# Three weight buffers, a lower part cast one piece later, and chains spread by one tile in a fused decoder layer

## The chip, the cores and the metric

The kernel runs on one core of a Trainium2 chip. The core has a matrix engine (PE, with its weight loads PEld), a vector engine (DVE), a scalar engine (ACT), a general engine (POOL), and a sync engine (SP) that here issues nearly all DMAs. Each engine runs its own instructions in the order in which the program was written, and waits where an operand is not ready. The metric is the device time of the core in microseconds (us); lower is better.

## The reference

One decoder layer on 256 tokens of width 2048, all in float32. A norm of x feeds one wide projection; three branches read it (gated linear attention, attention with a forget gate, attention into 256 memory tokens), each is gated, projected, gated again and summed, and an output projection is added to x.

```python
h = rmsnorm(x, norm_gain[l])
z = h @ w_in[l]
(gq, gk_, gv, ggate, gdown, fq, fk, fv, flogit, fgate,
 mq, mgate, merge) = jnp.split(z, IN_OFFSETS, axis=-1)
gk_log = log_sigmoid(gdown @ w_gk_up[l] + b_gk[l]) / GK_NORMALIZER
o_a = rmsnorm(gla_chunked(gq, gk_, gv, gk_log), gla_norm_gain[l]) * silu(ggate)
log_f = log_sigmoid(flogit + b_f[l])
o_b = forgetting_attention(fq, fk, fv, log_f) * silu(fgate)
mk, mv = jnp.split(rmsnorm(mem, mem_norm_gain[l]) @ w_mem_kv[l], 2, axis=-1)
o_c = memory_attention(mq, mk, mv) * silu(mgate)
y = (gates[:, :, 0] * (o_a @ wb[BRANCH_ROWS[0]:BRANCH_ROWS[1]])
     + gates[:, :, 1] * (o_b @ wb[BRANCH_ROWS[1]:BRANCH_ROWS[2]])
     + gates[:, :, 2] * (o_c @ wb[BRANCH_ROWS[2]:BRANCH_ROWS[3]]))
out = rmsnorm(x + y @ w_out[l], final_gain)
```

## The kernel before, in words

**Weights.** All large weights are one array `wall` of 34 blocks, each 2048 rows by 512 columns, in the order of use (`ORDER`): gq, gk, two blocks of gv, fq, fk, fv, the memory's key and value, mq, four gate blocks, then four times three merge blocks and a branch block, then four output blocks. A block has 16 row tiles of 128 rows. It is loaded in four quarters (four row tiles, 1 MB, tile `raw`, three buffers) and used in eight pieces (two row tiles each).

**Two parts.** A float32 product is made of three faster ones: each weight w is cast to a higher part (`hi`, an ACT cast, L131) and a lower part (`lo` = w - hi, a DVE subtraction, L132), four buffers each. x is split likewise into the tiles x12 (`split_x`, L298, ACT then DVE), the memory into m12.

**Pieces.** `w_split` (L147) writes, for each piece up to a given one, first the load of a quarter (`w_load`, L138), then the cast, then the subtraction. `w_kts` (L169) calls it three pieces ahead of the piece that PE is to use (`AHEAD = 3`).

**Blocks on PE.** `natural` (L182) has tokens on partitions: per row tile and half of the tokens three matmuls of 512 columns, 96 for a block. `transposed` (L197) has weight columns on partitions: per row tile and group c of 128 columns one matmul of 512 columns (hi with both parts of x) and one of 256 (lo), 128 for a block. It works in groups of four row tiles (two pieces), and in a group over c = 0 to 3. The first block (gq) goes row tile by row tile, with four banks of the pool att; the blocks gk, fq, fk, mk, mq, fgate and mgate go by groups, with four banks of the pool acc. Its banks are emptied by `join` (L381): an ACT copy (L384), then a DVE sum (L385).

**Side work.** Everything else is written as generators in three lanes: post (what follows a block), side and main. After each row tile (natural) or each c of a group (transposed), `pull()` lets every lane go one step; `yield n` lets a lane rest until n pulls later. So the order on each engine is fixed by where the pulls fall. `small` (L344) is the narrow projection (gdown and flogit, tile sm): its weights wsr are split on DVE (L359, L360) and multiplied in groups of row tiles (L366). `scale_first` (L444) makes the norm of x: `rms_of` (L248) loads x again, squares it on ACT (L259), `rsqrt` (L237) takes the root, `row_of` (L266) turns the column into a row with one matmul (L273), and then sm, gq and gk are scaled. `gla_decay` (L470) makes the decay from sm (matmul L480, log-sigmoid on ACT, a scan on DVE, L495). `gla_scores` (L506) makes products with the decay (L571 to L578), a matmul from them (L582), and then in four rounds keys and queries (L528, L539, L547, L596), score matmuls (L622) and masked copies (L636). `aug` (L669) scales fq and fk (L680). `fox` (L686) and `memory` (L766) are the two softmax attentions (waits at L734 and L778). `load_mem` (L308) loads and splits the memory.

**First block.** `first_piece` (L319) loads x and the weights of a piece of block 0 in small steps and splits both.

Of the kernel before, what the change touches and what calls it, by code (L numbers as in the profile page):

```python
# [10 lines left out]
F32 = mybir.dt.float32  # L11
# [40 lines left out]
AHEAD = 3  # L52
# [9 lines left out]
def body(ctx, tc, xT, memT, xn, memn, wall, wsm, wup, cst, fgain, out):  # L62
# [73 lines left out]
    done = [0, 0]  # L136
# [10 lines left out]
    def w_split(upto):  # L147

        while done[1] <= min(upto, 8 * N_STREAM - 1):
            n = done[1]  # L150
            q, s = divmod(n, 2)
            w_load(q + (2 if q >= 3 else 0))
            hi = wpool.tile([P, 2, NB], F32R, tag="hi", name=nm("hi"))
            lo = wpool.tile([P, 2, NB], F32R, tag="lo", name=nm("lo"))
            if q < 4:
                first_piece(q, s, raws[q], hi, lo)
            else:
                split_w(raws[q][:, 2 * s:2 * s + 2, :], hi, lo)
            parts[n] = (hi, lo)
            done[1] += 1  # L160
# [36 lines left out]
    def transposed(h, wsrc, evac, bank=acc, group=4):  # L197

        ps = [None] * 4
        held = []
        for item in wsrc:
            held.append(item)
            if len(held) < group:
                continue
            for c in range(4):
                if ps[c] is None:  # L210
                    ps[c] = bank()
                cs_ = slice(c * P, (c + 1) * P)
                for kt, hi, lo in held:
                    hk = h_of(h, kt)
                    MM(ps[c], lhsT=hi[:, cs_], rhs=hk.rearrange("p a s -> p (a s)"),  # L215
                       start=(kt == 0), stop=False, skip_group_check=True)
                    MM(ps[c][:, :S], lhsT=lo[:, cs_], rhs=hk[:, 0, :], start=False,  # L217
                       stop=(kt == KT - 1), skip_group_check=True)
# [4 lines left out]
            for _ in held if group < 4 else ():  # L223
                pull()
            held = []
        if group < 4:
            for c in range(3):
                evac(c, ps[c])

        def last():  # L230
            yield 1
            evac(3, ps[3])

        post.append(last())


    def rsqrt(r, m4, n):  # L237
# [5 lines left out]
        yield 2  # L243
# [22 lines left out]
    def row_of(col, row):  # L266

        dg = a2([P, NT, P])
        for t in range(NT):
            nc.vector.tensor_scalar(dg[:, t, :], ident, col[:, t:t + 1], None, ALU.mult)  # L270
        yield 1
        ps = att()
        MM(ps[:, :S], lhsT=ones, rhs=dg.rearrange("p t s -> p (t s)"), start=True, stop=True)  # L273
        yield 1
        nc.scalar.copy(row, ps[:, :S])
        yield 1
# [21 lines left out]
    def split_x(h, raw, k, gc):  # L298
        nc.scalar.activation(h[:, k, 0, :], raw, AF.Copy, scale=gc)
        nc.vector.scalar_tensor_tensor(out=h[:, k, 1, :], in0=raw, scalar=gc,  # L300
# [6 lines left out]

    def load_mem():  # L308
        for g in range(4):
# [3 lines left out]
            yield 5  # L313
            for k in range(4):
                kt = 4 * g + k
                split_x(m12[g], raw[:, k, :], k, cs[:, C_MGAIN + kt:C_MGAIN + kt + 1])
                yield 1

    def first_piece(g, s, raw, hi, lo):  # L319
# [5 lines left out]
        for k in range(0, 2, step):  # L325
# [6 lines left out]
            for j in range(ks.start, ks.stop):  # L332
                kt = 4 * g + j
                split_x(x12[g], xraws[g][:, j, :], j, cs[:, C_GAIN + kt:C_GAIN + kt + 1])
# [9 lines left out]
    def small():  # L344
# [7 lines left out]
        yield 2  # L352
        nc.sync.dma_start(wsr, wsm)
        nc.sync.dma_start(wup_s, wup)
# [26 lines left out]
    def join(r):  # L381

        def evac(c, p):
            nc.scalar.copy(r[:, c, :], p[:, S:])  # L384
            nc.vector.tensor_tensor(out=r[:, c, :], in0=p[:, :S], in1=r[:, c, :], op=ALU.add)  # L385
        return evac

# [4 lines left out]
    def proj_T(h, *then):  # L392

        r = a4([P, 4, S])
        transposed(h, w_kts(w_block(), 2), join(r))
# [4 lines left out]
    def scaled(row, by=1.0):  # L400
        def then(r):
            yield 1
            scale_T(r, row, by)
# [40 lines left out]
    def scale_first():  # L444
# [6 lines left out]
        scale_T(G["k"], xrow)  # L451
        yield 1

    def log_sigmoid(*args):
# [5 lines left out]
        yield 2  # L460
        for dst, u, tmp in args:
            nc.scalar.activation(tmp, tmp, AF.Ln, bias=1.0)
        yield 2
# [42 lines left out]
    def gla_scores():  # L506
# [66 lines left out]
        yield 1  # L573
        nc.scalar.activation(cd[:, :, 0, :], cd[:, :, 0, :], AF.Exp, scale=1.0 / 16)
        nc.scalar.activation(cd[:, :, 1, :], B4[:, :, 1, :], AF.Exp, scale=1.0 / 16)
        yield 2
# [10 lines left out]
        for li in range(len(STEPS) + 1):  # L587
# [18 lines left out]
            else:  # L606
# [3 lines left out]
                yield 1  # L610
# [3 lines left out]
                yield 1  # L614
                for half in range(2):
                    times_odd(Qs[half], half)
                yield 1
# [68 lines left out]
    def fox():  # L686
# [52 lines left out]
        for k in range(6):  # L739
# [5 lines left out]
            if 1 <= k < 5:  # L745
# [3 lines left out]
                for h in last:  # L749
                    moved(h)  # L750
            if k < 4:
# [11 lines left out]
                yield 1  # L763


    def memory():  # L766
# [6 lines left out]
        for h in range(6):  # L773
# [18 lines left out]
            if h < 4:  # L792
# [15 lines left out]
                yield 1  # L808
# [87 lines left out]
    mkT = proj_T(m12, scaled(mrow))  # L896
    mv = proj_N(m12, mcol)
    mqT = proj_T(x12, scaled(xrow))
# [227 lines left out]
```

## Time and profile before

| | us |
|---|---|
| median of 3 runs | 844.44 (843.75 to 846.35) |
| the profiled execution | 846.4 |
| its span, first to last instruction | 844.6 |
| PE busy in it | 811.8 |
| DVE busy | 500.7 |
| ACT busy | 404.3 |
| mean granted clock of PE | 0.984 |

In a row of the timeline stand the start from the span's begin, the duration, the engine (SPq is SP's queue), the line, the operation, what it writes and reads, the size and the count; in brackets the idle time of the engine before it and what ended it. A row of waits has the engine and line that waited, what it waited for, and the total, the count and the longest. Tiles named `a` and `b` come from two general pools; `x` is x12, `m` is m12.

### The profile page before, as it was taken

The page shows a single profiled execution, that of the slowest core. Times are in us where ns is not written, and L with a number is a line of the kernel's source. Part 1 is how long each engine was busy: PE and PEld are TensorE (multiplying, and loading weights), DVE is VectorE, ACT ScalarE, POOL GpSimd, SP SyncE. Part 2 cuts the span into 40 slices and gives each one's busy share as a digit, 9 for nine tenths or more (in the row PEclk, how much of TensorE's full clock was granted, in tenths as well). Part 3 has the DMA queues.
Part 4 walks back from the last instruction along what each step waited for, and adds up shares of the span by engine and source line. Part 5 has one row for each costly group of instructions (what it writes and reads, how often), then busy time and mean ns, then how long its engine had stood idle before and what let it go on. Part 6 is the DMA issues. An engine that isn't in the chain of part 4 may idle for free.

```text
span 844.6 us, 9971 instructions
## 1 busy us (share of the span) xinstructions
PE 811.8 (96%) x3892; PEld 678.3 (80%) x3892; DVE 500.7 (59%) x700; ACT 404.3 (48%) x551; POOL 22.1 (3%) x44
## 2 busy tenths in 40 slices
PE   8598979999999999999999999999999999999995
PEld 7486768888878788788888888888888888888885
DVE  6357678897485467567644654456445744475653
ACT  6355666554555346454544344444444444444541
POOL 7000001010000000000000000000000000000000
PEclk9799989999999999999999999999999999999998
DMA  8484347544344444355555555554555555558623
GB/s 302 178 303 167 132 175 262 188 150 156 144 150 150 150 162 180 110 196 192 194 185 187 194 194 199 200 186 170 194 197 199 198 178 187 191 192 305 242 100 100
DMA packets 27358, 157.14 MB, mean 186 GB/s; under 512 B 3216, under 2 KB 4640, under 8 KB 10416
## 3 DMA queue, kind: packets, MB, share of 16 engines
q1 hardware_dynamic: 27040, 156.48, 52.1%
q8 instruction: 30, 0.49, 0.2%
q14 instruction: 16, 0.13, 0.0%
q10 hardware_dynamic: 144, 0.02, 0.0%
q0 software_dynamic: 128, 0.02, 0.0%
HBM read 154.39 MB, written 2.10 MB: 185 GB/s over the span
## 4 chain that ended last, share of the span: by engine, by line
PE 65%; DVE 1%; ACT 0%; DVEq 0%; issue 0%; ACTq 0%
PE acc L193 15%; PE acc L192 15%; PE acc L191 15%; PE acc L215 4%; PE acc L1012 3%; PE acc L1011 3%; PE acc L1013 3%; PE acc L217 2%; PE att L778 0%; PE att L922 0%; PE att L796 0%; PE att L822 0%; PE att L734 0%; PE att L787 0%; DVE lo L132 0%; ACT hi L131 0%
## 5 line engine op out<-in xcount | busy, mean ns | idle before, releaser
L132 DVE TENSOR_TENSOR lo<-raw,hi 128x1024 fp32r<-128x1024 f32 (+2 forms) x269 | 322.0, 1207 | 275.6 <-ACT hi L131 275.0
L131 ACT CAST hi<-raw 128x1024 fp32r<-128x1024 f32 (+2 forms) x269 | 275.1, 1035 | 317.4 <-PE acc L193 240.2
L191 PE MATMUL acc<-hi,x 128*128 128x512 f32 x544 | 217.3, 399 | 0.5 <-DVE a L385 0.5
L192 PE MATMUL acc<-lo,x 128*128 128x512 f32 x544 | 213.0, 391 | 0.3 <-DVE lo L132 0.3
L193 PE MATMUL acc<-hi,x 128*128 128x512 f32 x544 | 213.0, 392 | 0.0
L215 PE MATMUL acc<-x,hi 128*128 128x512 f32 x384 | 138.2, 402 | 0.0
L191 PEld LDWEIGHTS acc<-hi,x 128*128 128x128 f32 x544 | 103.0, 189 | 22.4 <-DVE a L385 0.9
L193 PEld LDWEIGHTS acc<-hi,x 128*128 128x128 f32 x544 | 102.7, 189 | 21.9
L192 PEld LDWEIGHTS acc<-lo,x 128*128 128x128 f32 x544 | 103.0, 189 | 21.5 <-DVE lo L132 0.8
L217 PE MATMUL acc<-x,lo 128*128 128x256 f32 x384 | 107.5, 280 | 0.0
L215 PEld LDWEIGHTS acc<-x,hi 128*128 128x128 f32 x384 | 72.1, 188 | 16.8 <-issue 0.5
L217 PEld LDWEIGHTS acc<-x,lo 128*128 128x128 f32 x384 | 72.5, 189 | 0.2
L191 PE MATMUL acc<-hi,oT 128*128 128x512 f32 x128 | 49.8, 389 | 0.0
L192 PE MATMUL acc<-lo,oT 128*128 128x512 f32 x128 | 49.8, 389 | 0.0
L193 PE MATMUL acc<-hi,oT 128*128 128x512 f32 x128 | 49.8, 389 | 0.0
L1011 PE MATMUL acc<-hi,a 128*128 128x512 f32 x96 | 37.5, 391 | 0.0
L1012 PE MATMUL acc<-lo,a 128*128 128x512 f32 x96 | 37.5, 390 | 0.0
L1013 PE MATMUL acc<-hi,a 128*128 128x512 f32 x96 | 37.4, 389 | 0.0
L191 PEld LDWEIGHTS acc<-hi,oT 128*128 128x128 f32 x128 | 24.0, 188 | 5.0
L192 PEld LDWEIGHTS acc<-lo,oT 128*128 128x128 f32 x128 | 24.0, 188 | 5.0
L193 PEld LDWEIGHTS acc<-hi,oT 128*128 128x128 f32 x128 | 24.0, 188 | 4.9
L215 PE MATMUL att<-x,hi 128*128 128x512 f32 x64 | 24.0, 411 | 0.1
(214 smaller groups left out, 782.5 us busy)
## 6 DMA issues: line engine op xcount, KB each, us to landing
raw<-wall SPq DMA_DIRECT2D x132, 1024.0 KB, 4.7
a<-xn SPq DMA_DIRECT2D x8, 512.0 KB, 6.7
raw<-wall SPq DMA_DIRECT2D x4, 512.0 KB, 5.8
a<-memT SPq DMA_DIRECT2D x4, 512.0 KB, 5.6
a<-memn SPq DMA_DIRECT2D x4, 512.0 KB, 7.0
out<-a SPq DMA_DIRECT2D x8, 256.0 KB, 3.1
raw<-wall SPq DMA_DIRECT2D x7, 256.0 KB, 4.7
a<-xT SPq DMA_DIRECT2D x8, 128.0 KB, 4.3
```

The costliest lines, as they stand in the source:

```text
L131: cast(hi, src)
L132: nc.vector.tensor_tensor(out=lo, in0=src, in1=hi.bitcast(F32), op=ALU.subtract)
L191: MM(ps[t], lhsT=h1, rhs=hi, start=(kt == first), stop=False)
L192: MM(ps[t], lhsT=h1, rhs=lo, start=False, stop=False)
L193: MM(ps[t], lhsT=h2, rhs=hi, start=False, stop=(kt == last))
L215: MM(ps[c], lhsT=hi[:, cs_], rhs=hk.rearrange("p a s -> p (a s)"), start=(kt == 0), stop=False, skip_group_check=True)
L217: MM(ps[c][:, :S], lhsT=lo[:, cs_], rhs=hk[:, 0, :], start=False, stop=(kt == KT - 1), skip_group_check=True)
L1011: MM(ps, lhsT=h1, rhs=hi, start=(kt == 0), stop=False)
L1012: MM(ps, lhsT=h1, rhs=lo, start=False, stop=False)
L1013: MM(ps, lhsT=h2, rhs=hi, start=False, stop=(kt == KT - 1))
```

## The change

**Lower parts.** `w_split` becomes `w_cast` and `w_sub`. Casts stay three pieces ahead. The subtraction of a piece is written two pieces ahead in a natural block. In a transposed group it is written after the pulls of c = 0 and c = 2, and the two parts are those of the next group. The load of a quarter three further on follows the second subtraction of a quarter, which frees its raw buffer.

**Loads of the first blocks.** The second block's quarters are asked for after the last piece of the first block, not before its last quarter. The small weights' load moves from the lane into `first_piece`, after the second quarter.

**Norm.** `scale_first` enters the main lane before the first block with a rest of 11 pulls, and no longer scales gk: that follows gk's own block.

**Banks.** `join` is gone: copies and sums are written one c apart, the sum of a c after the copy of the next.

**Memory.** The cast and the subtraction of a row tile of the memory are one pull apart, the loads one quarter ahead; the memory's norm starts 24 pulls later.

**Chains.** In the root, the row, the log-sigmoid, the decay products, the last round of scores, fox and memory, one `yield` each is longer by one, or a `yield 1` is added.

```diff
-AHEAD = 3
-    def w_split(upto):
+    def w_cast(upto):
 
         while done[1] <= min(upto, 8 * N_STREAM - 1):
             n = done[1]
+            done[1] += 1
             q, s = divmod(n, 2)
-            w_load(q + (2 if q >= 3 else 0))
+            w_load(q)
             hi = wpool.tile([P, 2, NB], F32R, tag="hi", name=nm("hi"))
+            if q < 4:
+                lo = wpool.tile([P, 2, NB], F32R, tag="lo", name=nm("lo"))
+                first_piece(q, s, raws[q], hi, lo)
+                done[2] += 1
+                if n == 7:
+                    w_load(6)
+                parts[n] = [hi, lo]
+            else:
+                nc.scalar.copy(hi, raws[q][:, 2 * s:2 * s + 2, :])
+                parts[n] = [hi]
+
+    def w_sub(upto):
+
+        while done[2] <= min(upto, 8 * N_STREAM - 1):
+            n = done[2]
+            done[2] += 1
+            q, s = divmod(n, 2)
             lo = wpool.tile([P, 2, NB], F32R, tag="lo", name=nm("lo"))
+            nc.vector.tensor_tensor(out=lo, in0=raws[q][:, 2 * s:2 * s + 2, :], in1=parts[n][0].bitcast(F32),
+                                    op=ALU.subtract)
+            parts[n].append(lo)
+            if s == 1:
+                w_load(q + 3)
...
             if p % group == 0:
-                w_split(n + AHEAD)
+                w_cast(n + 3)
+            if group == 1:
+                w_sub(n + 2)
...
                 if group == 4:
                     pull()
-                    if held[-1][0] == KT - 1 and c:
-                        evac(c - 1, ps[c - 1])
+                    if c % 2 == 0:
+                        w_sub(8 * i + kt // 2 + 1 + c // 2)
+                    if kt == KT - 1:
+                        if c > 1:
+                            add(c - 2)
+                        if c:
+                            copy(c - 1)
...
+        if (g, s) == (1, 1):
+            nc.sync.dma_start(wsr, wsm)
+            nc.sync.dma_start(wup_s, wup)
...
-        yield 2
-        nc.sync.dma_start(wsr, wsm)
-        nc.sync.dma_start(wup_s, wup)
         yield 5
...
-    transposed(x12, w_kts(w_block()), join(gq), att, 1)
+    main.append(gap(11))
+    main.append(scale_first())
+    transposed(x12, w_block(), gq, att, 1)
     make_masks()
-    main.append(scale_first())
-    side.append(gap(8))
     side.append(load_mem())
+    side.append(gap(24))
     side.append(rms_of(memn, mcol, lambda: a4([P, 1024])))
     side.append(row_of(mcol, mrow))
-    G["k"] = proj_T(x12)
+    G["k"] = proj_T(x12, scaled(lambda: G["row"]))
```

Three places show what moves. The first is SP, the loads from the end of the first block's second quarter on (raw of 128x512 or 128x1024 is the first block, of 128x2048 a quarter of a later one). Before:

```order
L331 DMA raw_143<-wall 128x512
L328 DMA a_205<-xT 128x512
L331 DMA raw_202<-wall 128x1024
L353 DMA wsr<-wsm 128x384
L354 DMA wup_s<-wup 16x512
L328 DMA a_205<-xT 128x512
L331 DMA raw_202<-wall 128x1024
L144 DMA raw_260<-wall 128x2048
L144 DMA raw_262<-wall 128x2048
L328 DMA a_266<-xT 128x512
L331 DMA raw_259<-wall 128x1024
```

And in the change:

```order
L376 DMA raw_143<-wall 128x512
L384 DMA wsr<-wsm 128x384
L385 DMA wup_s<-wup 16x512
L373 DMA a_207<-xT 128x512
L376 DMA raw_204<-wall 128x1024
L373 DMA a_207<-xT 128x512
L376 DMA raw_204<-wall 128x1024
L373 DMA a_266<-xT 128x512
L376 DMA raw_263<-wall 128x1024
L373 DMA a_266<-xT 128x512
L376 DMA raw_263<-wall 128x1024
L143 DMA raw_315<-wall 128x2048
```

The two quarters of the second block (raw_260 and raw_262) stood ahead of the first block's last quarter (raw_259); now that quarter (raw_263) stands ahead of them, and the small weights (wsr) ahead of the third quarter.

The second is DVE where the first block's last quarter and the small weights (a_188, a_190) are split. Before:

```order
L132 TENSOR_TENSOR lo_234<-raw_202,hi_233 128x1024
L300 SCALAR_TENSOR_TENSOR x_38_267<-a_266,cs,x_38_267 128x256 x2
L132 TENSOR_TENSOR lo_265<-raw_259,hi_264 128x1024
L359 CAST a_188<-wsr 128x8x16
L360 TENSOR_TENSOR a_188<-wsr,a_188 128x8x16
L359 CAST a_188<-wsr 128x8x8
L360 TENSOR_TENSOR a_188<-wsr,a_188 128x8x8
```

And in the change:

```order
L131 TENSOR_TENSOR lo_234<-raw_204,hi_233 128x1024
L405 CAST a_190<-wsr 128x8x16
L406 TENSOR_TENSOR a_190<-wsr,a_190 128x8x16
L405 CAST a_190<-wsr 128x8x8
L406 TENSOR_TENSOR a_190<-wsr,a_190 128x8x8
L336 SCALAR_TENSOR_TENSOR x_36_267<-a_266,cs,x_36_267 128x256 x2
L131 TENSOR_TENSOR lo_265<-raw_263,hi_264 128x1024
```

The split of the first half of the small weights moved from behind the first lower part of the last quarter (lo_265) to ahead of it. On PE the eight matmuls that read it moved likewise, from behind 80 matmuls of the block to behind 64; the decay's first matmul moved from behind 292 matmuls of the large blocks to behind 268, the row of the norm of x from behind 268 to behind 248, the matmul of the decay products stays behind 388.

The third is DVE in the block of fk, third group (lo is a weight's lower part, the copies put scores into a mask, a_1424 and a_1437 are the next round's keys). Before:

```order
L636 COPY_PREDICATED a_863<-gmask,att_1405 128x8x24
L636 COPY_PREDICATED a_863<-gmask,att_1405 128x8x16
L636 COPY_PREDICATED a_863<-gmask,att_1405 128x8x8
L132 TENSOR_TENSOR lo_1422<-raw_1291,hi_1421 128x1024
L132 TENSOR_TENSOR lo_1426<-raw_1291,hi_1425 128x1024
L528 TENSOR_TENSOR a_1437<-a_828 128x1024
L539 TENSOR_TENSOR a_1456<-a_828 128x4x96
L539 TENSOR_TENSOR a_1456<-a_828 128x4x64
L539 TENSOR_TENSOR a_1456<-a_828 128x4x32
```

And in the change:

```order
L566 TENSOR_TENSOR a_1424<-a_821 128x1024
L172 TENSOR_TENSOR lo_1426<-raw_1251,hi_1412 128x1024
L278 TENSOR_TENSOR nwu_1406<-nwp_1405 128x2
L279 SCALAR_TENSOR_TENSOR nwu_1406<-nwu_1406,ms_1402 128x2
L280 SCALAR_TENSOR_TENSOR mcol<-nwu_1406,nwp_1405 128x2
L304 TENSOR_SCALAR b_1447<-ident,mcol 128x128 x2
L577 TENSOR_TENSOR a_1451<-a_821 128x4x96
L577 TENSOR_TENSOR a_1451<-a_821 128x4x64
L577 TENSOR_TENSOR a_1451<-a_821 128x4x32
L172 TENSOR_TENSOR lo_1455<-raw_1251,hi_1414 128x1024
```

The two lower parts stood together ahead of the next round's keys; now the second (lo_1455) stands behind the keys, the memory's norm and a set of queries.

More of the change, by code (lines that the diff above doesn't have):

```diff
@@ L135, in body @@
     raws, parts = {}, {}
-    done = [0, 0]
+    done = [0, 0, 0]
     def w_load(upto):
@@ L312, in load_mem @@
             nc.sync.dma_start(raw, memT[:, 4 * g:4 * g + 4, :])
[L313 to L317, printed above, removed]
+            yield 3
+            if g:
+                yield from split_mem(g - 1, old)
+            old = raw
+        yield 1
+        yield from split_mem(3, old)
     def first_piece(g, s, raw, hi, lo):
@@ L450, in scale_first @@
         yield 1
-        scale_T(G["k"], xrow)
-        yield 1
+        G["row"] = xrow
     def log_sigmoid(*args):
```

77 lines of the change are left out of this document (42 added, 35 removed).

## The prediction

> **What bounds the kernel now.** I read the page's first two parts, then what PE waits for, then the stretches around the waits.
>
> ```profile
> span 844.6 us, 9971 instructions
> PE 811.8 (96%) x3892; PEld 678.3 (80%) x3892; DVE 500.7 (59%) x700; ACT 404.3 (48%) x551; POOL 22.1 (3%) x44
> ...
> PE   8598979999999999999999999999999999999995
> ```
> PE is the bound, and for 33 us of the span it does nothing, by the slices (21 us each) mostly in the first six. The waits of PE (total, times, longest) say where:
>
> ```profile
> PE acc L366 <- DVE a L360: 8.7, 1, 8.7
> PE att L582 <- DVE a L578: 5.5, 1, 5.5
> PE att L273 <- DVE b L270: 3.5, 2, 2.6
> PE att L778 <- DVE b L791: 1.2, 1, 1.2
> PE att L734 <- DVE b L726: 1.2, 1, 1.2
> PE acc L191 <- DVE a L385: 0.5, 1, 0.5
> PE acc L192 <- DVE lo L132: 0.3, 1, 0.3
> ```
> The windows (length, PE, PEld, DVE, ACT, POOL busy, granted clock, DMA) show what a pause costs besides itself:
>
> ```profile
> 21.30:25.30 4.00, 0.06 (x1) 0.00 (x0) 0.06 (x1) 0.00 (x0) 0.00 (x0) 1.00 1.01 394
> 70.70:73.20 2.50, 0.44 (x2) 0.00 (x1) 2.39 (x7) 2.50 (x6) 0.00 (x0) 0.99 0.00 0
> 73.20:76.70 3.50, 3.00 (x7) 2.43 (x8) 3.50 (x8) 0.41 (x2) 0.00 (x0) 0.52 0.97 349
> 110.70:117.70 7.00, 6.00 (x18) 5.09 (x19) 4.74 (x6) 1.94 (x4) 0.00 (x0) 0.51 0.47 168
> 50.00:60.00 10.00, 10.00 (x58) 8.66 (x57) 4.72 (x4) 5.95 (x8) 0.00 (x0) 1.00 0.80 282
> 500.00:600.00 100.00, 100.00 (x447) 82.80 (x446) 52.19 (x49) 44.00 (x47) 0.00 (x0) 1.00 0.54 190
> ```
> The first row is the longest pause; behind the pause in the second row PE runs at half clock for 3.4 us, and for 7 us behind that for L582 (fourth). The last two rows give PE's pace at full clock: 10/58 = 0.172 us for a matmul of the transposed blocks, 100/447 = 0.224 us for one of 512 columns. From 400 to 800 us PE is full, and there I expect nothing.
>
> **Term A, the first block.** These rows of the timeline (start, duration) are the pause at 21 us:
>
> ```profile
> 13.21 2.34 SPq L144 DMA_DIRECT2D raw<-wall  x2
> 21.39 0.33 SPq L331 DMA_DIRECT2D raw<-wall  x1
> 17.56 0.39 PE L215 MATMUL att<-x,hi 128*128 128x512 f32 x1
> 18.53 0.39 PE L217 MATMUL att<-x,lo 128*128 128x256 f32 x1 [0.58 <-DVE lo L132]
> 19.05 1.05 ACT L131 CAST hi<-raw 128x1024 fp32r<-128x1024 f32 x1 [0.82 <-DMA raw<-wall]
> 20.14 1.22 DVE L132 TENSOR_TENSOR lo<-raw,hi 128x1024 fp32r<-128x1024 f32 x1 [0.87 <-ACT hi L131]
> 29.01 0.22 DVE L359 CAST a<-wsr 128x128 fp32r<-128x128 f32 x1
> 29.69 0.23 DVE L360 TENSOR_TENSOR a<-wsr,a 128x64 fp32r<-128x64 f32 x1
> 30.06 3.75 PE L366 MATMUL acc<-x,a 128*128 128x512 f32 x8 [8.70 <-DVE a L360]
> 43.92 0.40 PE L215 MATMUL acc<-x,hi 128*128 128x512 f32 x1
> ```
> Two loads of the second block go out at 13.21; the last quarter of the first block takes the raw buffer that is left and goes out at 21.39, when the lower part begun at 20.14 has freed it. The split of the small weights stands behind that quarter on DVE, and PE behind the split.
>
> In the change (order of SP) the last quarter follows the third at once, in a buffer long free. On DVE the first split now stands right behind the lower part that ends at 20.14 + 1.22 = 21.36; it takes 29.01 to 29.92, 0.9 us, so it ends at 22.3. On PE its eight matmuls come two row tiles earlier, so PE stops already at 17.6 and restarts at 22.3: a pause of 4.7 us, not of 8.7. From there 64 matmuls of the block (11.0 us) and all 16 small ones (3.6) remain: 36.9. The pause is longer than the one that lowered the clock at 73.2, so I add 3.4 us at half clock, 1.7 lost: the block ends at 38.6. Before it ended at 43.9 with four of the small matmuls still to come (0.9). **Gain 6.2 us**; 7.9 if the clock stays up, 4.5 if it is low for 6.8 us as at 110.7. The small weights' own load now stands ahead of the third quarter; PE waits for their split anyway.
>
> **Term B, the norm of x.** The pause of 2.6 us, the 0.5 us for a bank, and 3.4 us at half clock (1.7) make 4.8. The chain's loads, squares and root now start in the first block. These rows price it:
>
> ```profile
> 63.07 1.06 ACT L259 ACTIVATE a<-a 128x1024 f32<-128x1024 f32 x1
> 66.50 1.28 ACT L242 ACT_TABLE_LOAD   x1
> 68.16 0.51 ACT L299 ACTIVATE m<-a,cs 128x256 fp32r<-128x256 f32 x1
> 73.16 0.48 DVE L270 TENSOR_SCALAR b<-ident,xcol 128x128 f32<-128x128 f32 x2
> ```
> The last square stands on ACT behind two casts (2 x 1.05) that wait for PE to end the second block's second group, 64 x 0.172 = 11.0 us after 38.6. So 49.6 + 2.1 + 1.1 + 0.5 for a memory cast + 1.7 for the root with its table load + 1.0 on DVE (the two products, and as much again for three small steps, an estimate) = 56.0. PE comes to the row's matmul at 38.6 + 120 x 0.172 = 59.2: 3 us to spare. What is late next is the scaled small result: on DVE it stands behind a lower part (1.22) whose cast (1.05) waits for the second block's end, and PE wants it 12 matmuls (2.7 us) later: with the memory part and the scaling, 0.5 us late. **Gain 4.3**; 1.5 to 4.8.
>
> **Term C, the decay chain.**
>
> ```profile
> 106.31 0.63 ACT L574 ACTIVATE a<-a 128x512 f32<-128x512 f32 x1 [5.01 <-DVE a L571]
> 108.42 1.23 DVE L132 TENSOR_TENSOR lo<-raw,hi 128x1024 fp32r<-128x1024 f32 x1 [1.75 <-ACT hi L131]
> 110.96 0.69 DVE L578 TENSOR_TENSOR a<-a,a 128x512 f32<-128x512 f32 x1
> 99.98 2.29 DVE L495 TENSOR_TENSOR_SCAN a<-a,a 128x1024 f32<-128x1024 f32 x1
> ```
> PE waits 5.5 us for L578, then has 6.0 busy us at half clock (3.0 lost), and 0.3 for a lower part: 8.8. The chain now starts 24 matmuls (5.4 us) earlier in PE's order while L582's place stays, and its DVE steps no longer stand behind lower parts that wait for a cast (1.75 us in the second row): about 2 us to spare. The added pulls give each engine time between steps; what they delay is the chain, which has that 2 us. But a lower part is now queued two pieces (5.4 us) ahead of its use instead of three, and the scan (2.29) with its two neighbours stands in front of one: I count 0.8 us there and 0.5 on the next two. **Gain 7.5**; 3 to 8.8.
>
> **Term D, later chains.** The second L273 wait (3.5 - 2.6 = 0.9), L778 and L734 (1.2 each) each get one pull more, 1.4 us or longer: 3.3. I take **3.0**; 0 to 3.3.
>
> **Term E, the price.** In a transposed block the lower parts now stand behind the pulls of column groups 0 and 2, so the side work of DVE comes first. Before, both were at the front. Where DVE is fullest (fk, the fifth block):
>
> ```profile
> 164.10 0.68 DVE L680 SCALAR_TENSOR_TENSOR a<-a,xrow 64x512 f32<-64x512 f32 x1
> 164.70 0.94 DVE L636 COPY_PREDICATED a<-gmask,att 128x192 f32<-128x192 uint32 x3
> 170.02 2.36 DVE L132 TENSOR_TENSOR lo<-raw,hi 128x1024 fp32r<-128x1024 f32 x2 [0.68 <-ACT hi L131]
> 172.30 1.22 DVE L528 TENSOR_TENSOR a<-a 128x1024 f32<-128x1024 f32 x1
> 173.43 1.12 DVE L539 TENSOR_TENSOR a<-a 128x384 f32<-128x384 f32 x3
> ```
> From 5.1 us into the block (two lower parts, two sums, one product) DVE has 4 x 0.68, 4 x 0.94, three lower parts (3.5), 1.2, the memory norm's small steps with their two products (1.3, as in term B with the mean), 1.1 and the lower part in question (1.2): 14.8, so it ends at 19.9. PE wants it after 96 matmuls (16.5), eight score matmuls (1.3, an estimate from 192 columns of 512) and 0.9 for the group's first part: at 18.7. **Cost 1.2**; nothing if DVE packs tighter, 3.5 if the clock falls too. Elsewhere a lower part has 4 us or more of side room. Casts and subtractions are as many as before, and the loads, one quarter further ahead, keep their pace.
>
> **Sum.** 6.2 + 4.3 + 7.5 + 3.0 - 1.2 = 19.8. The profiled execution took 846.4 (span 844.6 and 1.8 around it): 826.6. It lies 2.0 above the median of 844.44, so the median comes to **824.6**.
>
> **Rivals.**
> *ACT takes the place of DVE* before L582: its exponentials stand behind casts and a table load (1.28). Against it: ACT is 48% busy; for it: L574 had waited 5.0 us, and now the wait is at its end. A pause of 3 us with 1.7 us of lost clock: 829.3. Chance 0.15.
> *DVE becomes the bound* in more of the transposed groups: four waits of 1.2 and one lowered clock, 6.5 instead of 1.2: 829.9. For it: DVE leaves little free where the scores run; against it: before, lower parts there were done some 4 us early. Chance 0.13.
> *The clock stays up* after the first pause. That needs a whole quiet stretch of 3.4 us to lower it: a pause of 4.7 us holds one in (4.7 - 3.4)/3.4 = 4 of 10 cases, and the other way the sum gains 1.7: 822.9. Against it: at 73.2 the clock fell after 2.5 us in which PE had still done 0.44. Chance 0.1.
> The Trainium skill, "TensorE: Matmul & The Clock Gate", section "Part 1: The HAM clock gate (the "warmup" mystery)", has this rule: half clock after at least one idle window of about 3.4 us, which runs freely. This trace agrees on the length of the low stretch (3.4 at 73.2) and not on the idle time that is needed.
> *Slower:* the second lower part of every group in the seven later transposed blocks (28 groups) comes late by as much as in term E. 28 x 1.2 = 33.6 against a gain of 21.0 without E: 857. It decides from 0.75 us a group, that is when such a part starts later than about 5.2 us into a group of 5.5. Against it: outside the scores DVE has under 3 us of other work a group. Chance 0.03.
> *No change:* A and C both turn into other waits of their old size, 843 to 846. Chance 0.02.
>
> **Numbers.** The forecast (821 to 828) has 0.57. All terms at their best give 819.6, at their worst 838.9; the rivals up to 830 belong in, so the range is 818.5 to 832. A measurement of this kernel can tell about 0.3% (2.5 us) from no change: faster 0.95, within 0.02, slower 0.03.
>
> **What would show it.** A: PE's pause near 18 us, 4 to 5 us long, ended by the small split, and the first matmul of the second block near 38 to 39. B: no wait for the row's matmul near 59. C: no wait over 1 us for the products of the decay, and the clock at full from 60 to 150 us. D: none of the three rows among the waits. E: one wait of 1 to 2 us for a lower part near 160 us. I am wrong if PE's pause at 18 us lasts 7 us, if a pause over 2 us remains between 60 and 130 us, or if waits for lower parts sum to over 5 us.

## The result, and the profile after

The changed kernel takes **838.72 us** (median of 4, 838.04 to 839.3) against 844.1 before in the same session: ratio 0.9932, 95% interval 0.9911 to 0.9952. The profiled execution took 839.3 us. So it is faster, by 5.4 us of the 19.8 that were forecast, and lies outside the range. Some executions of some kernels below were disturbed and ran far longer; the ratios leave them out.

The page's first two parts, after:

```profile
span 837.2 us, 9962 instructions
PE 809.4 (97%) x3892; PEld 678.0 (81%) x3892; DVE 499.5 (60%) x700; ACT 407.7 (49%) x553; POOL 21.8 (3%) x44
...
PE   7999999999999998999999999999999999999695
```

A slice is 21 us long. Before, PE's gaps stood in the first six slices. Now one stands in the third slice from the end. What PE waits for (total, times, longest):

```profile
PE acc L1052 <- DVE lo L172: 7.9, 1, 7.9
PE acc L412 <- DVE a L406: 4.3, 1, 4.3
PE acc L240 <- DVE b L881: 2.8, 1, 2.8
...
PE acc L210 <- DVE lo L172: 0.8, 1, 0.8
PE acc L242 <- DVE lo L172: 0.7, 1, 0.7
```

Of the old waits, those for the decay products, the rows and the two softmaxes (5.5, 3.5, 1.2, 1.2) are all gone, and the pause of the first block (8.7) is 4.3. Two new ones stand beside it: 7.9 and 2.8. The windows (length, PE, PEld, DVE, ACT, POOL busy, granted clock, DMA) add what each pause costs behind itself:

```profile
21.30:28.10 6.80, 6.07 (x16) 4.95 (x17) 5.17 (x13) 2.90 (x4) 1.06 (x2) 0.50 0.98 383
331.90:335.30 3.40, 3.40 (x12) 2.90 (x11) 0.85 (x3) 0.30 (x2) 0.00 (x0) 0.50 0.75 275
789.30:796.10 6.80, 3.22 (x8) 2.54 (x9) 5.77 (x5) 3.78 (x4) 0.00 (x0) 0.50 0.49 178
```

In each pause, or right behind it, PE's granted clock falls to half. At the first block's it stays there for 6.8 us (first row); the second row loses 1.7 us more, the third 1.6 (PE works for 3.2 of its 6.8 us). So the new waits cost 2.8 + 1.7 and 7.9 + 1.6, 14.0 us in all.

**The place at 331 us** (timeline; start, duration):

```profile
327.56 1.03 PE L835 MATMUL att<-a,a 128*128 128x256 f32 x4
328.62 0.69 DVE L837 TENSOR_REDUCE mmx<-att 128x2 f32<-128x512 f32 x1 [1.58 <-PE att L835]
329.43 1.22 DVE L172 TENSOR_TENSOR lo<-raw,hi 128x1024 fp32r<-128x1024 f32 x1
330.56 1.41 DVE L881 SCALAR_TENSOR_TENSOR b<-acc,xcol,b 128x512 f32<-128x512 f32 x2
331.36 0.50 PE L240 MATMUL acc<-x,hi 128*128 128x512 f32 x1 [2.78 <-DVE b L881]
```

The block of fgate wants its third bank, which L881, the product of the gate block before it, must empty. The sigmoid that L881 needs was done at 327.8 (ACT, 326.54 and 1.27 long). But on DVE L881 stands behind the memory attention's row maximum (L837), which reads a matmul that PE makes directly before it stops, and behind a lower part. The longer rests in `memory` and `fox` put L837 there: before, the product stood ahead of the maximum, and with the rests alone (t4, below) it stands behind it too. But with the rests alone PE waits only 0.3 us for it, so the 2.8 us take the rests and another part of the change; without the shift (e4, below) 1.6 are left.

**The place at 793 us**, where the last output block's weights (tiles lhi and llo, `late_loads`) are split among the stream's:

```profile
771.85 2.00 ACT L130 CAST lhi<-raw 128x1024 fp32r<-128x1024 f32 x2 [2.69 <-DMA raw<-wall]
772.93 2.36 DVE L131 TENSOR_TENSOR llo<-raw,lhi 128x1024 fp32r<-128x1024 f32 x2 [5.20 <-ACT lhi L130]
...
780.07 1.06 ACT L162 CAST hi<-raw 128x1024 fp32r<-128x1024 f32 x1 [1.15 <-DMA raw<-wall]
780.85 13.47 SPq L1071 DMA_DIRECT2D raw<-wall  x3
788.25 1.99 ACT L130 CAST lhi<-raw 128x1024 fp32r<-128x1024 f32 x2 [6.11 <-DMA raw<-wall]
789.33 2.36 DVE L131 TENSOR_TENSOR llo<-raw,lhi 128x1024 fp32r<-128x1024 f32 x2 [6.46 <-ACT lhi L130]
791.61 3.49 DVE L172 TENSOR_TENSOR lo<-raw,hi 128x1024 fp32r<-128x1024 f32 x3
792.88 0.80 PE L1052 MATMUL acc<-lo,a 128*128 128x512 f32 x1 [7.94 <-DVE lo L172]
```

The piece that PE waits for was cast at 780.07, so its lower part could have been ready at about 782.4. It comes at 792.8, because on DVE a split of the last block stands in front of it, whose own load went out at 780.85 and whose cast began at 788.25. The same had happened at the split before (first two rows: DVE idle for 5.2 us up to 772.93), which kept back the lower parts behind it until 775.21, and with them the raw buffers that they free. Before, the lower part stood in front of such a split:

```profile
796.50 1.23 DVE L132 TENSOR_TENSOR lo<-raw,hi 128x1024 fp32r<-128x1024 f32 x1 [0.25 <-ACT hi L131]
800.54 2.36 DVE L132 TENSOR_TENSOR llo<-raw,lhi 128x1024 fp32r<-128x1024 f32 x2 [0.74 <-ACT lhi L131]
```

DVE's order at this place, before and after (without numbers of tiles that do not matter):

```
before: lo (a piece)  lo (next piece)  ...  llo x2         lo
after:  lo (a piece)  ...              llo x2  lo (next piece)  lo
```

### The profile page after: what moved, and what is told of

Read it like the earlier page. It is cut to its first block, busy times and chain, and to the rows that moved or that the text cites. A ratio compares the mean times of both kernels' runs of the same rounds, so it can differ in the third digit from the quotient of the medians.

```text
span 837.2 us, 9962 instructions
## 1 busy us (share of the span) xinstructions
PE 809.4 (97%) x3892; PEld 678.0 (81%) x3892; DVE 499.5 (60%) x700; ACT 407.7 (49%) x553; POOL 21.8 (3%) x44
## 4 chain that ended last, share of the span: by engine, by line
PE 89%; DMA 4%; DVE 3%; ACT 2%; SPq 1%; issue 1%; DVEq 0%; ACTq 0%
PE acc L209 19%; PE acc L211 18%; PE acc L210 18%; PE acc L240 12%; PE acc L242 6%; DMA raw<-wall 4%; PE acc L1052 3%; PE acc L1053 3%; PE acc L1051 3%; PE att L660 1%; PE att L240 1%; DVE lo L172 1%; ACT hi L162 1%; PE acc L412 1%; PE att L242 0%
## 5 line engine op out<-in xcount | busy, mean ns | idle before, releaser
L172 DVE TENSOR_TENSOR lo<-raw,hi 128x1024 fp32r<-128x1024 f32 x256 | 311.9, 1223 | 204.5 <-ACT hi L162 204.3
L162 ACT CAST hi<-raw 128x1024 fp32r<-128x1024 f32 x256 | 266.1, 1052 | 327.7 <-PE acc L211 244.7
L210 PE MATMUL acc<-lo,x 128*128 128x512 f32 x544 | 212.2, 390 | 0.8 <-DVE lo L172 0.8
L240 PE MATMUL acc<-x,hi 128*128 128x512 f32 x384 | 140.4, 408 | 2.8 <-DVE b L881 2.8
L210 PEld LDWEIGHTS acc<-lo,x 128*128 128x128 f32 x544 | 102.3, 188 | 21.8 <-DVE lo L172 1.2
L240 PEld LDWEIGHTS acc<-x,hi 128*128 128x128 f32 x384 | 72.9, 190 | 19.9 <-DVE b L881 3.2
L210 PE MATMUL acc<-lo,oT 128*128 128x512 f32 x128 | 49.9, 390 | 0.0
L1051 PE MATMUL acc<-hi,a 128*128 128x512 f32 x96 | 38.1, 397 | 0.0
L1052 PEld LDWEIGHTS acc<-lo,a 128*128 128x128 f32 x96 | 18.4, 192 | 12.6 <-DVE lo L172 8.8
L210 PEld LDWEIGHTS acc<-lo,oT 128*128 128x128 f32 x128 | 24.0, 188 | 5.0
```

The lines of the kernel that those rows point to most:

```text
L162: nc.scalar.copy(hi, raws[q][:, 2 * s:2 * s + 2, :])
L172: nc.vector.tensor_tensor(out=lo, in0=raws[q][:, 2 * s:2 * s + 2, :], in1=parts[n][0].bitcast(F32), op=ALU.subtract)
L210: MM(ps[t], lhsT=h1, rhs=lo, start=False, stop=False)
L1051: MM(ps, lhsT=h1, rhs=hi, start=(kt == 0), stop=False)
L1052: MM(ps, lhsT=h1, rhs=lo, start=False, stop=False)
```

## Experiments: the two new waits

The first four kernels, e1 to e4, start from the changed kernel, and their diffs are against it.

**e1, lower parts ahead of the last block's splits.**

```diff
@@ late_loads
+            w_sub(done[1] - 1)
             for s in range(2):
                 split_w(raw[:, 2 * s:2 * s + 2, :], hi[:, 2 * s:2 * s + 2, :], lo[:, 2 * s:2 * s + 2, :])
```

> The changed kernel, with the lower parts whose casts are already written put ahead of each split of the last output block on DVE (the place they had before the change). Theory 'DVE queue': the 8.1 us wait of PE at 793 us is a lower part that stands behind the last block's split, which waits for its load; in front of it the wait goes, with the 3.4 lost at half clock after it being 1.6 to 3.4: PE's wait for a lower part in the out blocks falls below 1 us, time 838.7 - 9.7 = 829 (828 to 831). Theory 'raw buffers': with loads one quarter further ahead the last block's loads find none of the three buffers free, whatever DVE's order: the wait stays at 6 us or more, time 837 to 839.

Measured: 830.0 us, ratio to before 0.9835 (0.9804 to 0.9866), 8 us less than the change by the ratios. PE's wait in the output blocks:

```profile
PE acc L1052 <- DVE lo L172: 1.1, 1, 1.1
```

It fell from 7.9 to 1.1, a touch over the forecast of 1, and the clock stayed up. The theory of DVE's queue holds; the loads, three quarters ahead as in the change, did not keep the wait alive.

**e2, the gate's product ahead of the memory's maximum.**

```diff
@@ silu_gate
                 nc.scalar.activation(sgs[t], ps[t], AF.Sigmoid, scale=xcol[:, t:t + 1])
-            yield 2
+            yield 1
```

> The changed kernel, with the product that empties the gate's banks (L881) written one pull earlier, so that on DVE it stands ahead of the memory attention's row maximum (L837) and of a lower part. Theory 'longer chains': the 2.8 us wait of PE at 331 us comes from L837, which reads a matmul that PE has only just made, standing in front of L881: the wait goes below 0.5 us and the clock stays up at 332, time 838.7 - 2.8 - 1.7 = 834.2 (833.5 to 835.5). Rival 'ACT late': the sigmoid with its table load ends too late for the bank in any order: a wait of over 1.5 us stays there, time 837 to 839.

Measured: 835.0 us, ratio 0.9881 (0.9851 to 0.9912), 4 us less than the change. No row of L240 for L881 is left among PE's waits, and PE runs at full clock from 331.8 to 335.3. The sigmoid was not the cause.

**e3, both.**

> Both edits at once: the lower parts ahead of the last block's splits, and the gate's product ahead of the memory's maximum. If the two give-backs are independent the gains add: 838.7 - 9.7 - 4.5 = 824.5 (823 to 826), which is the sum of the prediction. If a PE that is earlier at 331 us only meets later DMA or DVE limits, it stays at 827 or above.

Measured: 828.59 us, ratio 0.9814 (0.9778 to 0.9850); its profiled execution took 825.93. Four executions lie between 825.93 and 831.87, so the expected 823 to 826 is met by the lowest and missed by the median. The two edits together give 10 us by the ratios where 14.2 were expected. Part of the missing 4 goes with the clock: the two quicker executions (825.93 and 827.29) ran at a mean clock of 0.992 and 0.993, the two others (829.89 and 831.87) at 0.991 and 0.988. What PE still waits for:

```profile
PE acc L412 <- DVE a L406: 3.8, 1, 3.8
...
PE acc L1052 <- DVE lo L172: 1.1, 1, 1.1
PE acc L210 <- DVE lo L172: 0.8, 1, 0.8
PE acc L242 <- DVE lo L172: 0.7, 1, 0.7
```

This is the list that the prediction expected of the change: the first block's pause, and small waits for lower parts.

**e4, lower parts right behind their casts again.**

```diff
@@ w_kts
                 w_cast(n + 3)
-            if group == 1:
-                w_sub(n + 2)
+                w_sub(n + 3)
```

> The changed kernel with every lower part written right behind its cast again, three pieces ahead; the loads stay three quarters ahead and all else stays changed. Theory 'DVE queue': the wait at 793 us goes (a lower part is again in front of the last block's split), the two small waits at 88 and 157 us go (0.9 each), and the wait for the gate's bank at 331 shrinks by the lower part of 1.2 us that stood in front of it, to about 1.6, still with half clock; the decay chain loses part of its room, 1 to 3 us: time 838.7 - 9.7 - 1.8 - 1.2 + 2 = 828 (826 to 831). Theory 'raw buffers': the wait at 793 stays at 6 us or more, as the loads are as far ahead as in the change: 836 to 838. If the split of casts and lower parts is what the gain at 60 to 120 us rests on, a wait of 4 us or more for the decay products is back: 832 or above with the wait at 793 gone.

Measured: 847.76 us, ratio 1.0036 (1.0018 to 1.0055): 20 us above the forecast, and slower than before the change. The bank's wait at 331 us did shrink to 1.6, as expected, and of the 7.9 us in the output blocks 4.0 are left, in shorter waits. New are above all the rows that wait for L227 and L615:

```profile
PE acc L239 <- DVE a L227: 3.0, 2, 2.6
PE acc L208 <- DVE a L227: 2.9, 2, 1.9
PE att L619 <- DVE a L615: 2.8, 1, 2.8
PE acc L1051 <- DVE lo L172: 2.3, 2, 1.1
PE acc L1050 <- ACT hi L162: 1.7, 1, 1.7
PE acc L239 <- DVE b L880: 1.6, 1, 1.6
```

L227 is the sum that empties a bank of a transposed block. Its timeline shows what holds it:

```profile
143.86 2.36 DVE L172 TENSOR_TENSOR lo<-raw,hi 128x1024 fp32r<-128x1024 f32 x2 [2.57 <-ACT hi L162]
146.14 0.42 DVE L227 TENSOR_TENSOR a<-acc,a 128x256 f32<-128x256 f32 x1
146.70 0.47 PE L239 MATMUL acc<-x,hi 128*128 128x512 f32 x1 [2.60 <-DVE a L227]
```

Two lower parts wait 2.57 us for their casts, and the sum, ready long before, waits behind them. So the shift is not a mere side matter of the change: it keeps a wait for ACT out of DVE's queue. Without it the banks cost 5.9 us, where the kernel before had 0.5. The 2.8 for L619 is the wait for the decay products, which the expectation feared at 4 or more. The rows of L1051 and L1050 also show that the output blocks lose 4.0 us when loads three quarters ahead meet lower parts at their casts; s3, below, has the same pair of waits. So the rival was not all wrong, though it is not what makes the 7.9.

## Experiments: the parts alone

Each of these starts from the kernel before and takes one part of the change.

**s1, the shift of the lower parts**: `w_split` becomes `w_cast` and `w_sub` as in the change, but the load stays where it was, ahead of the cast and two quarters ahead.

```diff
-                w_split(n + AHEAD)
+                w_cast(n + AHEAD)
+            if group == 1:
+                w_sub(n + 2)
...
                     pull()
+                    if c % 2 == 0:
+                        w_sub(8 * cur[0] + held[-1][0] // 2 + 1 + c // 2)
```

> The kernel before with one part of the change alone: lower parts written one piece (in transposed blocks, two pulls) behind their casts; loads two quarters ahead, banks, norm and chains as before. The prediction saw here only a price (1.2 us) and some room for the decay chain (about 2 us). Theory 'the lower parts carry the gain': undoing them in the changed kernel cost 17.8 us against the version with the last block mended (847.8 against 830.0), so here the waits between 60 and 350 us shrink by 5 us or more, and the wait for a lower part behind the last block's split appears (6 to 9 us, near 800): time about 844.1 - 7 + 9.7 = 847 (844 to 850). Rival 'only together': without the chains' room the lower parts give nothing, and the price and the late wait remain: 844.1 + 1.2 + 9.7 = 855 (852 to 857). If loads three quarters ahead are needed for the late wait, that is absent and the time is 837 (first) or 845 (second).

Measured: 846.2 us, ratio 1.0014 (0.9999 to 1.0029), not clear of no change and in the range of the first theory (844 to 850).

```profile
PE acc L1031 <- DVE lo L172: 7.8, 2, 7.5
PE att L601 <- DVE a L597: 2.6, 1, 2.6
```

The wait for the decay products (5.5 before) is halved, and the 7.5 us wait in the output blocks is there, with loads only two quarters ahead. The shift alone makes it. It also makes a wait of 2.0 us for a lower part in a natural block, at 97 us.

**s2 and t4, the longer rests** (the same kernel twice; the diff adds one to each `yield` named in the change, or the `yield 1` in `fox`).

> The kernel before with the longer rests in the chains alone (root, row, log-sigmoid, decay products, last score round, fox, memory). By the prediction they take 3.0 us of waits (second L273, L734, L778) and part of the 8.8 at the decay products. Theory 'queue': the chains end later and stand behind lower parts that wait for a cast, so L582's wait (5.5 us) does not shrink, and the wait for the gate's bank of about 1.6 us with half clock appears near 345: 844.1 - 3 + 3.3 = 844.4 (842 to 847). By the prediction: 841 or below, without that wait.

> The kernel before with the longer rests alone, once more, for an undisturbed profile: 833 to 836. If the rests work by giving each chain more PE work between its matmuls, the waits for L273, L582, L734 and L778 (11.4 us before) are all below 0.5, the clock falls only behind the first pause, and no wait for the gate's bank is over 1 us, since there the lower part stands ahead of its cast's wait; the waits left are the 8 us of the first block.

Measured: 834.78 us, ratio 0.9882 (0.9862 to 0.9902), and 834.05 in one further execution. Of the first expectation, the theory (842 to 847) was missed; the reading by the prediction (841 or below, without the bank's wait) held, with 6 us more than it named. The second expectation had the time, but two of its waits are not below 0.5, and the clock fell once more, at 111 us. From the trace of that further execution:

```profile
PE acc L366 <- DVE a L360: 7.7, 1, 7.7
PE att L582 <- DVE a L578: 1.8, 1, 1.8
...
PE att L273 <- DVE b L270: 0.6, 1, 0.6
```

The four waits of 11.4 us before are 2.4, and the bank's wait for the gate's product is 0.3. Rests alone make more than the whole change does. What they change is a distance: in the order of PE (equal neighbours counted once) the matmul of the decay products stands 98 instructions behind the decay's first matmul before the change, and 122 with the rests. The chain has 24 more matmuls of cover. The distance is not all that counts: s1 has 98 and waits 2.6, e4 has 122 and waits 2.8.

**s3, the loads and the small weights.**

```diff
-            w_load(q + (2 if q >= 3 else 0))
+            w_load(q)
...
                 first_piece(q, s, raws[q], hi, lo)
+                if n == 7:
+                    w_load(6)
             else:
                 split_w(raws[q][:, 2 * s:2 * s + 2, :], hi, lo)
+                if s == 1:
+                    w_load(q + 3)
...
+        if (g, s) == (1, 1):
+            nc.sync.dma_start(wsr, wsm)
+            nc.sync.dma_start(wup_s, wup)
...
-        yield 2
-        nc.sync.dma_start(wsr, wsm)
-        nc.sync.dma_start(wup_s, wup)
         yield 5
```

> The kernel before with the loads alone: the second block's behind the first's, the small weights' load after the second quarter and its matmuls two row tiles earlier, quarters three ahead. By the prediction term A, 6.2 us; with the low clock of 6.8 us seen in the changed kernel, 4.5: time 838 to 840, the pause near 18 us 4 to 5 us long. Rival: what is gained at 38 us meets the norm's chain, which stands where it was and waits for its own loads: PE's wait for the row's matmul (2.6 us before) grows to 6 or more and the time is 842 to 844.

Measured: 855.62 us, ratio 1.0134 (1.0110 to 1.0159): worse than even the rival had it.

```profile
PE att L277 <- DVE b L274: 6.6, 2, 4.0
...
PE acc L370 <- DVE a L364: 3.6, 1, 3.6
PE acc L195 <- DVE a L389: 3.1, 2, 2.2
PE acc L1016 <- DVE lo L132: 1.9, 2, 1.1
PE acc L1015 <- ACT hi L131: 1.7, 1, 1.7
```

The pause of the first block did fall (8.7 to 3.6). The gain went, in part as the rival said, to the rows of the norms (3.5 to 6.6, x's row 4.0 of it) and to the banks (0.5 to 3.1), and then the output blocks lose 3.6 that they did not lose before.

**s4, the norm**: `gap(11)` and `scale_first` ahead of the first block, gk scaled behind its own block, `gap(24)` ahead of the memory's norm, as in the change's last hunk; the `gap(8)` ahead of the memory's load, which the change drops, stays.

> The kernel before with the norm alone: its loads, squares and root begun in the first block, gk scaled after its own block, the memory's norm 24 pulls later. By the prediction term B, 4.3 us, and 3 to 5 us of C, as the decay chain starts 24 matmuls earlier: 836 to 838. Rival: the chain's DVE steps still stand behind lower parts that wait for casts, so L582's wait shrinks by 2 us at most, and only B is seen: 839 to 841. If the norm's loads take bandwidth from the last quarter of the first block, the pause at 21 us grows by up to 5 us (2 MB at some 390 GB/s) and nothing is gained: 842 to 846.

Measured: 846.09 us, ratio 1.0013 (0.9997 to 1.0028). Nothing is gained. Only the third expectation has the time, and its reason is not the one: the pause at 21 us is 8.4, not longer than before.

```profile
PE att L581 <- DVE a L577: 5.7, 1, 5.7
PE att L273 <- DVE b L270: 4.9, 1, 4.9
```

The first row's wait (2.6) is gone, but the wait for the decay products is what it was: the whole chain, its matmul of products included, moved forward by some 30 instructions, and the distance is still 98. The 4.9 is the memory's row, near 191 us.

**t3, the change without the rests** (all `yield`s of s2 taken back in the changed kernel).

> The changed kernel with the rests in the chains as before (all else changed). Theory 'the rests carry the gain': they alone made 9.7 us, so without them the waits for decay products, rows and scores are back (5 us or more together between 60 and 350) and the bank wait at 331 us goes: 838.7 + 9.7 - 4.5 = 844 (841 to 847). Rival 'lower parts and norm carry it', as the prediction had it for the decay products: no wait over 1 us there, and only the three rows of term D return: 838.7 + 3.3 - 4.5 = 837.5 (836 to 839).

Measured: 838.71 us, ratio 0.9940 (0.9924 to 0.9956): the time of the change itself.

```profile
PE att L307 <- DVE b L304: 2.9, 1, 2.9
PE att L620 <- DVE a L616: 1.7, 1, 1.7
```

The time lies in the rival's range (836 to 839), but not by the rival's waits: it had none over 1 us for the decay products. Without the rests the shift still keeps the decay products at 1.7, the memory's row costs 2.9, and the bank's wait at 331 us is gone. Inside the whole change the rests give about as much as they take at 331 us.

## Experiments: the first block

**t1, both mends, and the small matmuls later** (on top of e3).

```diff
@@ small
-        yield 5
+        yield 3
         for g in range(2):
...
-            yield 1
+        yield 6
         sp = acc()
-        for kts, n in ((range(0, 8), 3), (range(8, 12), 4), (range(12, 16), 1)):
+        for kts, n in ((range(0, 8), 3), (range(8, 12), 3), (range(12, 16), 1)):
```

> The version with both give-backs mended (828.6), and in the first block the split of the small weights written two row tiles earlier on DVE and their matmuls two row tiles later on PE. Term A took the pause before these matmuls as the price of the last loads. Theory 'order on PE': at 17.6 us PE has the ninth row tile's weights at 19.1, and the small matmuls stand in front of it; with them later the pause falls to 1.5 to 2.5 us, the clock stays at full, and the first matmul of the second block is at 34 to 35 instead of 38 to 40. 3 us of it may return at the row's matmul of the norm: 828.6 - 5.5 + 1.5 = 824.6 (822 to 827). Rival 'DMA': the loads of the first block set its end (6 MB and the small weights), the pause only moves behind the ninth row tile and stays over 4 us: 827 to 829.

Measured: **820.22 us**, ratio 0.9719 (0.9701 to 0.9736), the fastest kernel here and below both forecasts. The waits in the first block are now 1.1 for a cast and 1.1 for lower parts, and none returns at the norm's row. In the execution with the trace (824.31 us) the second block begins at 36.4, not at 34 to 35, since the clock fell all the same (windows):

```profile
16.70:20.10 3.40, 1.50 (x8) 0.82 (x6) 1.47 (x3) 2.26 (x4) 0.00 (x0) 1.00 0.99 378
20.10:23.50 3.40, 3.40 (x11) 2.92 (x12) 3.26 (x11) 3.31 (x6) 0.00 (x0) 0.51 1.04 416
```

It fell once more at 781.3 us, and this execution's mean clock is 0.992. PE is busy through both stretches, so they lose 1.7 us each, 3.4 of the 4.1 us between this execution and the median. The four others took 819.78 to 820.33 at 0.996 to 0.997. The half clock at the end of the span (6.6 us in the trace) makes 0.996 by itself, so these four had no room for another stretch of 3.4 us: there the clock stayed full up to the end, as the theory had it.

**t2, the rests and the first block's part on the kernel before** (loads of the second block behind the first's, then two quarters ahead; rests of s2; `small` as in t1).

> The kernel before with the longer rests (834.8 alone) and the first block's part: second block's loads behind the first's, two quarters ahead from then on, the small split early and its matmuls late; no shift of lower parts, no earlier norm. If the parts add: 834.8 - 9 (block one ends near 35 instead of 43.9) = 826, with no wait near 800 us. Rival from the loads alone (855.6): the gain of the first block is given back at the norm's row matmul and at the bank of the second block near 62 to 70 us, as the norm's own loads come no earlier: 830 to 835.

Measured: 824.32 us, ratio 0.9765 (0.9747 to 0.9782), 1.7 below the forecast. With neither the shift nor the earlier norm it is 14 us faster than the change. What s3 gave back is not given back here, and at mean clocks of 0.996 to 0.997 the executions of 823 to 825 us leave no room for a stretch at half clock before the end. That the rests cover the norms' rows, and that loads two quarters ahead leave the output blocks alone, is argued from the times; the waits of such an execution are in no trace. Which of the two carries more was not tried.

## Why the prediction was wrong, step by step

**The step that failed** is "From 400 to 800 us PE is full, and there I expect nothing", and with it "Elsewhere a lower part has 4 us or more of side room" (term E). Term E looked for side work of DVE that stands ahead of a shifted lower part, and priced it by its busy time. It missed the place where an instruction that *waits* stands ahead: the last block's split waits for its load, and PE waited 7.9 us for the lower part behind that split. The second place has the same mechanism, but what waits there is the gate's product behind the row maximum, which waits for PE; it belongs to term D, which counted a gain for the rests and no price. With their half clock the two places cost 9.5 and 4.5 in the profile.

Putting the orders back gave 8 us (e1), 4 us (e2) and 10 us (e3) of the 14.1 by which the forecast was off. The first place comes from the shift alone (s1); the second is gone without the rests (t3), and is 0.3 with nothing but the rests (t4). What remains, some 4 us, is partly the clock: e3's quickest execution, 825.93 us, had 6.8 us at half clock in the first block where the prediction took 3.4, and two others ran at a lower mean clock still. The rest is not settled. One of the prediction's own signs did show it: the waits for lower parts sum to over 5 us (7.9, 0.8 and 0.7).

**Term A** was right in kind: a pause of 4.3 us (4.7 forecast), ended by the small split. The half clock lasted 6.8 us, not 3.4: the prediction took the 3.4 from the pause at 73 us, while the pause in the first block itself had 10.2 us at half clock before the change (25.4 to 35.6). So the second block began at 39.9, not 38.6: 4.1 us earlier than before, with the four small matmuls 5.0 instead of 6.2. But s3 shows that this gain is not the loads' own. Alone they cost 11 us; other parts of the change cover what then becomes late. And "PE waits for their split anyway" (of the small weights) was too quick: t1 shows that PE had other work.

**Term B**: no wait for the row's matmul near 59, as forecast. It was wrong to count it as a gain of its own: the norm alone gives nothing (s4).

**Term C**: the whole wait of 5.5 went, the clock stayed full from 60 to 150, and the 0.8 us for a lower part behind the scan came as computed (the row of L210, at 88 us). The reason was only half right. The prediction set the gain on the chain's earlier start "while L582's place stays". By the parts, the start gives nothing (5.7 left in s4); the place stays because the rests push it back by as much as the norm pulls it forward. The rests leave 1.8, the shift 2.6.

**Term D**: the three rows are gone, 3.3 us. At 331 us the rests had a price of 4.5 that the prediction did not count.

**Term E** in the block of fk: forecast one wait of 1.2 near 160 us; it was 0.7 at 157.

**The rivals.** None of them had the two waits. The nearest was the slower one, with a lower part behind DVE's other work, but at the wrong places: the 28 groups of the transposed blocks show one wait of 0.7. The rival of the clock asked for a whole quiet stretch of 3.4 us; by the last section half a stretch is enough.

## What to carry to other kernels

An instruction that is written later on an in-order engine changes its neighbours everywhere in the program, also where PE is full before: go through the whole order for instructions ahead of it that wait for a load or for another engine, and price those by when their operand comes, not by their length. Where a dependent chain sets a wait, first give it more distance (rests cost one number each and made 9.7 us here alone), and check what the moved steps then stand in front of. Parts of a schedule change do not add: alone they came to about +1.7, -9.7, +11.2 and +1.6 us (the first and the last not clear of no change), together to -5.4 (the banks' order and the memory's split, not tried alone, are in the last figure only).

## What the runs showed of the hardware

The clock does not need a pause to fall. In every trace its changes lie a whole number of stretches of 3.41 us apart. In t1's trace PE was busy for 1.50 of the 3.40 us ahead of 20.1, in no wait longer than 1.1 us, and the next stretch ran at half clock. Its second fall, and the emptiest stretch that is not followed by one (t3, at 88.7 us), lie close together (first two rows t1, last two t3):

```profile
777.91:781.32 3.41, 1.67 (x6) 1.02 (x6) 3.41 (x4) 2.65 (x3) 0.00 (x0) 1.00 0.33 70
781.32:784.73 3.41, 3.41 (x10) 2.62 (x9) 1.25 (x2) 0.72 (x1) 0.00 (x0) 0.50 0.96 401
88.70:92.11 3.41, 1.71 (x13) 1.23 (x11) 3.41 (x6) 3.04 (x5) 0.00 (x0) 1.00 0.47 135
92.11:95.53 3.42, 3.42 (x18) 2.82 (x17) 3.42 (x5) 2.33 (x4) 0.00 (x0) 1.00 0.43 182
```

So here a stretch of 3.41 us counts as idle with 1.67 us of work in it (49%) and not with 1.71 (50%); in the other traces at full clock every fall, and every such stretch inside the span without one, agrees with these bounds. The Trainium skill, "TensorE: Matmul & The Clock Gate", section "Part 1: The HAM clock gate (the "warmup" mystery)", asks for an idle window of about 3.4 us; these rows agree with the window's length, and show that it may hold work. The way back has bounds too: half clock ended behind a stretch with 2.86 us of work (before, at 73.2) and went on behind one with 2.65 (the change, at 21.3). So the price of much the same pause of the first block differs by its place on the grid: 6.8 us at half clock after 4.3 us in the change, 3.4 us after 5.0 us in e1, whose first half-clock stretch held 2.96 us of work.
